# Scores of dilated attention made for two heads together, on the two halves of the partitions

## The chip, the cores and the metric

The kernel runs on one core of a Trainium2 chip. The metric is the time of one execution on the device in microseconds (us). A run is compared by the median of several executions. In the profile the engines are PE (TensorE; PEld is its loading of weights), DVE (VectorE), ACT (ScalarE), POOL (GpSimd) and SP (SyncE, which issues the DMAs).

## What is computed

A decoder trunk of two layers on 256 positions of width 1024, in float32. Each layer is

```python
h = rmsnorm(x, norm1_g[l])
z = h @ w_in[l]
out_a = dilated_mixture(qa, ka, va)          # 3 groups x 4 heads of 64, strides 1, 4, 16
out_b = diff_attention(qb, kb, vb, lam, ...) # 4 heads with two score maps each
out_c = multiscale_pool(z[..., OFF_C:OFF_G], pool_w[l], pool_scale[l])
mixed = (gates[:, :, 0] * (out_a @ w_proj_a[l])
         + gates[:, :, 1] * (out_b @ w_proj_b[l])
         + gates[:, :, 2] * (out_c @ w_proj_c[l]))
x = x + mixed @ w_out[l]
h2 = rmsnorm(x, norm2_g[l])
x = x + (swiglu(h2, ...) if l % 2 == 0 else moe_ffn(h2, ...))   # 8 experts, top 2
```

The dilated mixture makes, for each of four output heads, three maps of scores (one per group), masks them, and mixes the three softmax results by their denominators.

## The kernel before

Every weight matrix is loaded in pieces of 1 MB (tile `raw`), and each piece is split into a high part on ACT (`wh`, line 204) and a low part on DVE (`wl`, line 220). A product of float32 precision is then three matmuls of 128x128 by 128x512 (`mm3`, lines 299 to 301). Half a piece is 12 such matmuls. `run_plan` walks through a list: for each half it first converts the half that lies four ahead (`convert`), then issues the 12 matmuls, then calls `step_bg` once. All instructions of an engine run in the order in which this program writes them.

`step_bg` lets in side jobs. A side job is a generator; `bg` holds them in the order of their priority (a low number first). Each call may advance up to three of them (`st["rate"]`), each to its next `yield ready(lag, when, ...)`: it may go on after `lag` more halves, when its condition holds, and when the places that it asks for are free. The places are counted by `CAPS`: 4 PSUM buffers `tmp`, 6 probability tiles `P`, 3 transposed ones `PT`, 2 jobs of dilated attention `A`, 2 of differential attention `B`.

In a layer's mixer the plan makes the queries and keys of dilated attention first. The rotary embedding runs as a side job (`rope_T`: DVE works on `zq`, PE transposes at line 675, ACT copies to `qk` at line 679). A tile `qk` holds two heads, one on partitions 0 to 63 and one on 64 to 127. Then come the four jobs `attn_a(h)`. Each does, with a `yield` between: three blocks of `scores` (lines 698 and 699, a contraction over the 64 partitions of its half), `mask_max` (line 705, DVE), exponentials (line 711, ACT), transposes of the three probability tiles (line 716, PE), their copies to `PT` (line 721, ACT), the products with the values (lines 766 to 769, PE) and the weighted sum (lines 777 and 779, DVE). `attn_a_tail` transposes the result. Meanwhile the plan goes on through the other projections of `z`. The jobs `attn_b(h)` of differential attention follow with a lower priority; one of them makes two score maps, on the two halves of the same tiles `qk`. `attn_b_tail` takes the reciprocal root (`rsqrt`, lines 353 to 367, 12 operations of DVE on 8 columns), scales (line 875), transposes (line 882, PE) and splits (lines 309 on ACT and 315 on DVE) into `outB`. The pooling's job `pool_c` runs between them.

At the end of the mixer stand the projections of the three branches. Those of the pooling (two halves, key `outC`) and of dilated attention (one half, key `outA`) come first, for both halves of the columns, into buffers `acc`: 72 matmuls. Behind each DVE mixes the result in (line 923, or lines 926 and 928). Then `finish_bg()` issues all that is left of the side jobs, and the projection of differential attention follows into buffers `tmp`. The layer's rest (`w_out`, the norm, the dense part or the experts) depends on it.

The functions that the change touches:

Of the kernel before, what the change touches and what calls it, by code (L numbers as in the profile page):

```python
# [89 lines left out]
def trunk(ctx: ExitStack, tc: tile.TileContext, coff, cst, x, positions, norm1_g, w_in, b_gate, diff_lambda,  # L90
# [7 lines left out]
    RA, RB, WA, WB, LROPE, LC, TAB, LBT = 3, 3, 1, 2, 2, 2, 2, 1  # L98
    CAPS = {"tmp": 4, "P": 6, "PT": 3, "A": 2, "B": 2}
    AHEAD, AHEAD2 = 4, 3  # L100
# [12 lines left out]
    def tmp():  # L113
        return pp[0].tile([128, 512], F32, tag="tmp", name="tmp")
# [113 lines left out]
    def ready(lag=1, when=None, **holds):  # L228

        return lag, when, holds  # L230

    def add_bg(name, gen, prio=5):
        it = [name, gen, prio, 0, None, {}, {}]
        bg.append(it)
        bg.sort(key=lambda t: t[2])
        advance(it)

    def advance(it):
        it[5] = it[6]
        try:  # L240
            lag, when, holds = next(it[1]) or ready()
            it[3], it[4], it[6] = st["half"] + lag, when, holds
        except StopIteration:
            bg.remove(it)
# [102 lines left out]
    def small(n, name, dt=F32, bufs=2):  # L347
        return sp.tile([128, n], dt, tag=name, name=name, bufs=bufs)
# [125 lines left out]
    def first_group(ps, bank, start=False, func=None):  # L474
# [4 lines left out]
        def fn(get, j):  # L479
# [25 lines left out]
            if start:  # L505
                tables = rope_tables()
                inv_rms(lambda: next(tables))
                add_bg("tables", rest(tables), 0)
            else:
                inv_rms()  # L510
# [71 lines left out]
    def mixer(l):  # L582
        L = {}
        lam_init = 0.8 - 0.6 * math.exp(-0.3 * l)

        def mt(shape, tag, bufs=1, dt=F32):
            return (mp if tag in ("qk", "gate") else mpa).tile(shape, dt, tag=tag, name=tag, bufs=bufs)
# [69 lines left out]
        def ev_qk(key, nb):  # L657
            def f(ps):
                if L.get("rope", 0) >= 2:
                    finish_bg(f"rope{L['rope'] - 2}")  # L660
                z = mt([128, NT, 512], "zq", 2)
                to_sbuf([z[:, 0], z[:, 1]], ps)
                add_bg(f"rope{L.get('rope', 0)}", rope_T(key, nb, z), 1)
                L["rope"] = L.get("rope", 0) + 1
            return f
# [28 lines left out]
        def scores(qt, kt, par):  # L694

            r = slice(par * 64, par * 64 + 64)
            p = tmp()
            PE.matmul(p[:, 0:128], qt[r, 0:128], kt[r, 0:128], start=True, stop=True)
            PE.matmul(p[:, 128:384], qt[r, 128:256], kt[r, 0:256], start=True, stop=True)
            return p  # L700

        def mask_max(p, mask, m0, m1):
            P = mt([128, 384], "P", 6)
            for a, b, m in ((0, 128, m0), (128, 384, m1)):
                V.tensor_tensor_reduce(P[:, a:b], p[:, a:b], mask[:, a:b], 1.0, -3.0e38,
                                       op0=OP.add, op1=OP.max, accum_out=m)
            return P

        def exps(P, nm, ls):
            for (a, b), n_, s_ in zip(((0, 128), (128, 384)), nm, ls):  # L710
                S.activation(P[:, a:b], P[:, a:b], AF.Exp, bias=n_, scale=SCALE, accum_out=s_)

        def transpose3(P):
            p = tmp()
            for j in range(3):
                PE.transpose(p[:, j * 128:(j + 1) * 128], P[:, j * 128:(j + 1) * 128], ident)
            return p

        def evac3(p):
            t = mt([128, 384], "PT", 3)  # L720
            S.activation(t, p[:, :384], AF.Copy)
            return t

        def attn_a(h):
            yield ready(0, lambda: len(L.get("qa", [])) == 6, tmp=3, A=1)
            pr, par = divmod(h, 2)
            if h == 0:
                L["oa"] = mt([128, NT, 256], "oa")
            ps = []
            for g in range(3):  # L730
                hq, hk = 4 * g + h, AH + 4 * g + h
                ps.append(scores(L["qa"][hq // 4][:, (hq // 2) % 2], L["qa"][hk // 4][:, (hk // 2) % 2], par))
            L["nA"] = L.get("nA", 0) + 1
            yield ready(1, P=3, A=1)
            m = small(6, "am")
            P = [mask_max(ps[g], masks[g], m[:, g:g + 1], m[:, 3 + g:4 + g]) for g in range(3)]
            m3 = m.rearrange("p (i g) -> p i g", g=3)
            M = small(2, "aM")
            V.tensor_reduce(M, m3, axis=AX.X, op=OP.max)
            nm = small(6, "anm")  # L740
            V.tensor_scalar(nm, m, -SCALE, None, op0=OP.mult)
            d = small(6, "ad")
            V.tensor_tensor(d.rearrange("p (i g) -> p i g", g=3), m3, M[:, :, None].to_broadcast([128, 2, 3]), op=OP.subtract)
            yield ready(1, P=3, A=1)
            ls = small(6, "al")
            for g in range(3):
                exps(P[g], [nm[:, g:g + 1], nm[:, 3 + g:4 + g]], [ls[:, g:g + 1], ls[:, 3 + g:4 + g]])
            e = small(6, "ae")
            S.activation(e, d, AF.Exp, scale=SCALE)
            yield ready(WA, tmp=3, A=1)  # L750
            pts = [transpose3(P[g]) for g in range(3)]
            yield ready(1, PT=3, A=1)
            pts = [evac3(p) for p in pts]
            w = small(6, "aw")
            V.tensor_tensor(w, e, ls, op=OP.mult)
            den = small(2, "aden")
            V.tensor_reduce(den, w.rearrange("p (i g) -> p i g", g=3), axis=AX.X, op=OP.add)
            V.reciprocal(den, den)
            c = small(6, "ac")
            V.tensor_tensor(c.rearrange("p (i g) -> p i g", g=3), e.rearrange("p (i g) -> p i g", g=3),  # L760
                            den[:, :, None].to_broadcast([128, 2, 3]), op=OP.mult)
            yield ready(1, tmp=1, A=1)
            o = tmp()
            for g in range(3):
                v = L["va"][:, :, (4 * g + h) * 64:(4 * g + h + 1) * 64]
                PE.matmul(o[:, g * 64:g * 64 + 64], pts[g][:, 0:128], v[:, 0], start=True, stop=True)
                ob = o[:, 192 + g * 64:256 + g * 64]
                PE.matmul(ob, pts[g][:, 128:256], v[:, 0], start=True, stop=False)
                PE.matmul(ob, pts[g][:, 256:384], v[:, 1], start=False, stop=True)
            yield ready()  # L770
            for i in range(NT):
                dst = L["oa"][:, i, h * 64:(h + 1) * 64]
                for g in range(3):
                    src = o[:, i * 192 + g * 64:i * 192 + (g + 1) * 64]
                    cc = c[:, i * 3 + g:i * 3 + g + 1]
                    if g == 0:
                        V.tensor_scalar(dst, src, cc, None, op0=OP.mult)
                    else:
                        V.scalar_tensor_tensor(dst, src, cc, dst, op0=OP.mult, op1=OP.add)

        def attn_a_tail():
            yield ready(1, lambda: not any(pending(f"A{h}") for h in range(4)), tmp=1)
            L["outA"] = pieces(mp, "qk", 10, 2)
            p = tmp()
            for k in range(2):
                for i in range(NT):
                    PE.transpose(p[:, k * 256 + i * 128:k * 256 + (i + 1) * 128],
                                 L["oa"][:, i, k * 128:(k + 1) * 128], ident)
            yield ready()
            split(*L["outA"].pieces[0], p.rearrange("p (k t) -> p k t", k=2))  # L790
# [147 lines left out]
        for b in range(3):  # L938
            z_block(b * 512, 512, ev_qk("qa", b))
            if b == 0:  # L940
                do(loads)
                do(lambda: add_bg("lam", lam(), 1))
                if l == DEPTH - 1:
                    do(router_loads)
            if b == 2 and l == DEPTH - 1:
                do(router_consts)
# [1 line left out]
        z_block(OFF_VA + 512, 256, ev_nat("va", 768, 512))  # L948

        def start_a():  # L950
            for h in range(4):
                add_bg(f"A{h}", attn_a(h), 3)
            add_bg("Atail", attn_a_tail(), 3)
            st["rate"] = RA

        def start_b():
# [3 lines left out]
            st["rate"] = RB  # L960

        do(start_a)
        z_block(OFF_QB, 512, ev_qk("qb", 0))
        z_block(OFF_KB, 512, ev_qk("kb", 0))
# [636 lines left out]
    masks = []  # L1601
# [91 lines left out]
```

## Time and profile before

| | |
|---|---|
| median of 3 runs | 1717.09 us (1716.28 to 1717.39) |
| the profiled execution | 1715.65 us, span 1713.9 us |
| PE busy | 1638.7 us, 96% of the span |
| DVE busy | 972.3 us, 57% |
| ACT busy | 798.4 us, 47% |
| DMA | 489.06 MB, mean 285 GB/s |

The span runs from the first to the last instruction. The first layer's mixer lies in about the first 275 us, the dense part up to 520, the second layer's mixer up to 775, and the experts behind it, with the DMA queues at about 400 GB/s.

### The profile page before, as it was taken

Reading aid. Unit: us, or ns where it says so; the run is one execution under the profiler, and the core shown is the slowest. Engines: PE = TensorE matmul, PEld = TensorE weight load, DVE = VectorE, ACT = ScalarE, POOL = GpSimd, SP = SyncE. Lnnn points to the kernel's source line nnn. Section 1 sums busy time; section 2 is a strip of 40 time slices with the busy share of each in tenths; the row PEclk is TensorE's granted clock in tenths of the full one; section 3 lists DMA queues with packets and bytes.
Section 4 is the critical chain, followed back from the end, with each engine's and each line's share of the span. In section 5 each row is a group of like instructions: output and inputs, shape, how many; then the busy total and the mean of one; then the engine's idle time right before and its main releaser. Section 6 shows DMA issues by size and latency. Waiting matters only on the chain. (4 is left out here: it accounts for less than half of the span.)

```text
span 1713.9 us, 24266 instructions
## 1 busy us (share of the span) xinstructions
PE 1638.7 (96%) x7753; PEld 1178.1 (69%) x7753; DVE 972.3 (57%) x1415; ACT 798.4 (47%) x994; POOL 3.1 (0%) x6
## 2 busy tenths in 40 slices
PE   9999999999999999998999999999999999999895
PEld 6878888888888888785575654766646666467464
DVE  6556686545456556684472644744536556257376
ACT  6555544443345555533452633635325544145362
POOL 0000000000000000000000000000000000000000
PEclk9999999999999999998999999999999999999997
DMA  8435555554546535485999989999899999999890
GB/s 270 165 123 168 171 185 194 178 205 170 198 153 194 172 126 164 159 319 221 410 410 407 407 339 413 406 399 405 335 411 403 399 407 374 381 411 410 327 398 28
DMA packets 161694, 489.06 MB, mean 285 GB/s; under 512 B 13424, under 2 KB 18672, under 8 KB 147440
## 3 DMA queue, kind: packets, MB, share of 16 engines
q1 hardware_dynamic: 161520, 486.86, 75.4%
q8 instruction: 94, 1.54, 0.4%
q14 instruction: 80, 0.66, 0.1%
HBM read 485.78 MB, written 1.05 MB: 284 GB/s over the span
## 5 line engine op out<-in xcount | busy, mean ns | idle before, releaser
L220 DVE TENSOR_TENSOR wl<-raw,wh 128x1024 fp32r<-128x1024 f32 (+1 forms) x407 | 671.0, 1670 | 347.1 <-ACT wh L204 328.4
L204 ACT ACTIVATE wh<-raw 128x1024 fp32r<-128x1024 f32 (+1 forms) x407 | 563.9, 1416 | 298.6 <-PE gu L301 78.6
L299 PE MATMUL acc<-wl,hTh 128*128 128x512 f32 (+1 forms) x544 | 218.7, 402 | 1.2 <-DVE wl L220 1.1
L301 PE MATMUL acc<-wh,hTl 128*128 128x512 f32 (+1 forms) x544 | 212.0, 390 | 0.4 <-DVE hTl L315 0.4
L300 PE MATMUL acc<-wh,hTh 128*128 128x512 f32 (+1 forms) x544 | 211.6, 389 | 0.0
L299 PE MATMUL gu<-wl,xg 128*128 128x512 f32 x448 | 180.9, 404 | 28.7 <-DVE wl L220 20.7
L1385 PE MATMUL gu<-raw,xf 128*64 128x512 f32 (+1 forms) x1016 | 200.8, 543 | 4.9 <-PEq L1301 4.9
L301 PE MATMUL gu<-wh,xg 128*128 128x512 f32 x448 | 177.4, 396 | 0.0
L300 PE MATMUL gu<-wh,xg 128*128 128x512 f32 x448 | 177.4, 396 | 0.0
L1385 PEld LDWEIGHTS gu<-raw,xf 128*64 128x64 f32 x1016 | 70.7, 137 | 110.6 <-issue 97.7
L299 PEld LDWEIGHTS gu<-wl,xg 128*128 128x128 f32 x448 | 84.6, 189 | 65.2 <-ACT wh L204 23.1
L299 PEld LDWEIGHTS acc<-wl,hTh 128*128 128x128 f32 x544 | 102.5, 188 | 27.1 <-issue 4.6
L301 PEld LDWEIGHTS acc<-wh,hTl 128*128 128x128 f32 x544 | 102.4, 188 | 24.2 <-DVE hTl L315 0.9
L300 PEld LDWEIGHTS acc<-wh,hTh 128*128 128x128 f32 x544 | 102.7, 189 | 20.3
L1385 PE MATMUL y<-raw,af 128*64 128x512 f32 x448 | 101.1, 596 | 0.0
L301 PEld LDWEIGHTS gu<-wh,xg 128*128 128x128 f32 x448 | 84.7, 189 | 20.0
L299 PE MATMUL y<-wl,aT 128*128 128x512 f32 x224 | 90.2, 403 | 8.0 <-DVE wl L220 7.2
L300 PEld LDWEIGHTS gu<-wh,xg 128*128 128x128 f32 x448 | 84.8, 189 | 18.2
L299 PE MATMUL tmp<-wl,cols 128*128 128x512 f32 x240 | 95.8, 399 | 0.0
L301 PE MATMUL tmp<-wh,cols 128*128 128x512 f32 x240 | 95.2, 397 | 0.0
L300 PE MATMUL tmp<-wh,cols 128*128 128x512 f32 x240 | 95.1, 396 | 0.0
L301 PE MATMUL y<-wh,aT 128*128 128x512 f32 x224 | 88.5, 395 | 0.0
(258 smaller groups left out, 1740.7 us busy)
## 6 DMA issues: line engine op xcount, KB each, us to landing
raw<-in_moe_w_up SPq DMA_DIRECT2D x112, 1024.0 KB, 10.7
raw<-in_moe_w_gate SPq DMA_DIRECT2D x111, 1024.0 KB, 11.2
raw<-in_moe_w_down SPq DMA_DIRECT2D x110, 1024.0 KB, 11.4
raw<-in_w_in SPq DMA_DIRECT2D x57, 1024.0 KB, 5.1
raw<-in_ffn_w_gate SPq DMA_DIRECT2D x14, 1024.0 KB, 5.2
raw<-in_ffn_w_up SPq DMA_DIRECT2D x14, 1024.0 KB, 5.2
raw<-in_ffn_w_down SPq DMA_DIRECT2D x14, 1024.0 KB, 5.1
raw<-in_w_out SPq DMA_DIRECT2D x8, 1024.0 KB, 5.2
```

Source lines behind the costliest of these rows:

```text
L204: S.activation(hi, raw_t[u][0][:, o:o + n], AF.Copy)
L220: V.tensor_tensor(lo, raw, hi.bitcast(F32), op=OP.subtract)
L299: PE.matmul(ps, xh, wl, start=start, stop=False)
L300: PE.matmul(ps, xh, wh, start=False, stop=False)
L301: PE.matmul(ps, xl, wh, start=False, stop=stop)
L1385: PE.matmul(ps[j * 64:j * 64 + 64, cols.start + o:cols.start + o + g], w, raw[:, kk, o + j * g:o + j * g + g], start=fst, stop=lst)
```

## The change

`scores_a(h)` for h = 0 and 2 makes the scores of heads h and h + 1 in turn for each of the three groups, two at a time, with a `yield` after each pair, and masks each pair one step later. It asks for both places `A` and for six tiles `P` in the end. When all three pairs are masked it adds the two jobs `attn_a(h, P, m)`, which go on from the maxima as before. `add_bg` lets a new job hold places from its start.

```diff
-    def add_bg(name, gen, prio=5):
+    def add_bg(name, gen, prio=5, **holds):
+
         it = [name, gen, prio, 0, None, {}, {}]
         bg.append(it)
         bg.sort(key=lambda t: t[2])
         advance(it)
+        it[5] = holds
...
-        def attn_a(h):
-            yield ready(0, lambda: len(L.get("qa", [])) == 6, tmp=3, A=1)
-            pr, par = divmod(h, 2)
+        def scores_a(h):
+
+            yield ready(0, lambda: len(L.get("qa", [])) == 6, tmp=2, A=2)
             if h == 0:
                 L["oa"] = mt([128, NT, 256], "oa")
-            ps = []
+            m = [small(6, "am") for _ in range(2)]
+            P = [[], []]
             for g in range(3):
                 hq, hk = 4 * g + h, AH + 4 * g + h
-                ps.append(scores(L["qa"][hq // 4][:, (hq // 2) % 2], L["qa"][hk // 4][:, (hk // 2) % 2], par))
-            L["nA"] = L.get("nA", 0) + 1
-            yield ready(1, P=3, A=1)
-            m = small(6, "am")
-            P = [mask_max(ps[g], masks[g], m[:, g:g + 1], m[:, 3 + g:4 + g]) for g in range(3)]
+                ps = [scores(L["qa"][hq // 4][:, (hq // 2) % 2], L["qa"][hk // 4][:, (hk // 2) % 2], j) for j in range(2)]
+                yield ready(1, P=2 * g + 2, tmp=2 if g < 2 else 0, A=2)
+                for j in range(2):
+                    P[j].append(mask_max(ps[j], masks[g], m[j][:, g:g + 1], m[j][:, 3 + g:4 + g]))
+            L["nA"] = L.get("nA", 0) + 2
+            for j in range(2):
+                add_bg(f"A{h + j}", attn_a(h + j, P[j], m[j]), 3, P=3, A=1)
+
+        def attn_a(h, P, m):
...
-            for h in range(4):
-                add_bg(f"A{h}", attn_a(h), 3)
+            for h in (0, 2):
+                add_bg(f"A{h}", scores_a(h), 3)
```

The program has as many instructions on PE as before, and those of SP and POOL stand in the same order. Side jobs move. In the rows of the changed program the lines stand 2 further down than before up to `start` of the dilated jobs (the scores are lines 700 and 701), and 7 further behind it (the scaling is line 882, the transposes 889).

**TensorE at the first scores** (`acc` is an ordinary projection, `tmp<-qk` a score map; a map is a row of 128 and a row of 256 columns). Before:

```order
L301 MATMUL acc<-wh,hTl 128x512
L698 MATMUL tmp<-qk 128x128
L699 MATMUL tmp<-qk 128x256
L698 MATMUL tmp<-qk 128x128
L699 MATMUL tmp<-qk 128x256
L698 MATMUL tmp<-qk 128x128
L699 MATMUL tmp<-qk 128x256
L299 MATMUL acc<-wl,hTh 128x512
```

And with the change:

```order
L303 MATMUL acc<-wh,hTl 128x512
L700 MATMUL tmp<-qk 128x128
L701 MATMUL tmp<-qk 128x256
L700 MATMUL tmp<-qk 128x128
L701 MATMUL tmp<-qk 128x256
L301 MATMUL acc<-wl,hTh 128x512
```

Before, a block is three maps of one head, and there are four such blocks in a layer. Now a block is two maps, of two heads, and there are six. Differential attention's maps, which stood in one block of four and two of two, now stand in four of two.

**ScalarE at the probabilities of the first two heads** (`P,al` are the exponentials of a head, `PT` the copies of transposed probabilities, `wh` conversions). Before:

```order
L749 ACTIVATE ae<-ad 128x6
L204 ACTIVATE wh<-raw 128x1024
L655 ACTIVATE zq<-acc,rr_267 128x512 x2
L711 ACTIVATE P,al<-P,anm 128x128
L711 ACTIVATE P,al<-P,anm 128x256
L711 ACTIVATE P,al<-P,anm 128x128
L711 ACTIVATE P,al<-P,anm 128x256
L711 ACTIVATE P,al<-P,anm 128x128
L711 ACTIVATE P,al<-P,anm 128x256
L749 ACTIVATE ae<-ad 128x6
L204 ACTIVATE wh<-raw 128x1024
L721 ACTIVATE PT<-tmp 128x384 x3
```

And with the change:

```order
L756 ACTIVATE ae<-ad 128x6
L713 ACTIVATE P,al<-P,anm 128x128
L713 ACTIVATE P,al<-P,anm 128x256
L713 ACTIVATE P,al<-P,anm 128x128
L713 ACTIVATE P,al<-P,anm 128x256
L713 ACTIVATE P,al<-P,anm 128x128
L713 ACTIVATE P,al<-P,anm 128x256
L756 ACTIVATE ae<-ad 128x6
L204 ACTIVATE wh<-raw 128x1024 x2
L681 ACTIVATE qk<-tmp 128x512
L723 ACTIVATE PT<-tmp 128x384 x3
```

The exponentials of the second head now follow those of the first at once, and two conversions and the copy of rotated queries (line 681) stand between them and the first head's copies.

**VectorE at the end of the first mixer** (`rr` is the reciprocal root's result, `nat<-gate,acc` and the pairs `gate`, `nat` mix a branch in, `zq<-zq,rr` is the scaling ahead of the transposes, `cols<-tmp,sg` the low part behind them). Before:

```order
L367 TENSOR_SCALAR rr_2026<-rr_2026 128x8
L220 TENSOR_TENSOR wl<-raw,wh 128x1024
L875 TENSOR_TENSOR zq<-zq,rr_2026 128x512 x2
L220 TENSOR_TENSOR wl<-raw,wh 128x1024
L923 SCALAR_TENSOR_TENSOR nat<-gate,acc 128x512 x2
L220 TENSOR_TENSOR wl<-raw,wh 128x1024
L926 SCALAR_TENSOR_TENSOR gate<-gate,acc 128x512
L928 TENSOR_TENSOR nat<-nat,gate 128x512
L926 SCALAR_TENSOR_TENSOR gate<-gate,acc 128x512
L928 TENSOR_TENSOR nat<-nat,gate 128x512
L315 SCALAR_TENSOR_TENSOR cols<-tmp,sg,cols 128x512
```

And with the change:

```order
L369 TENSOR_SCALAR rr_2124<-rr_2124 128x8
L220 TENSOR_TENSOR wl<-raw,wh 128x1024
L933 SCALAR_TENSOR_TENSOR gate<-gate,acc 128x512
L935 TENSOR_TENSOR nat<-nat,gate 128x512
L933 SCALAR_TENSOR_TENSOR gate<-gate,acc 128x512
L935 TENSOR_TENSOR nat<-nat,gate 128x512
L882 TENSOR_TENSOR zq<-zq,rr_2124 128x512 x2
L317 SCALAR_TENSOR_TENSOR cols<-tmp,sg,cols 128x512 x2
```

Before, the four mixing operations shown are those of the first half of the columns. With the change they are those of the second half, behind the last matmuls into `acc`; the mixing of the second pooled half, four rows for two sums of squares and the other 11 operations of the root stand right ahead of the first row shown. On TensorE the 8 transposes, which stood in two blocks of 4 with 24 matmuls into `acc` between them and 24 behind, now stand in one block, behind all matmuls into `acc` and right ahead of those into `tmp`. The product of the last head with the values stands 36 matmuls ahead of that block; it stood 48 ahead of the first block and 96 ahead of the matmuls into `tmp`.

## Rows read from the trace of the kernel before

**Rows 1.** Busy time by windows: both mixers; granted clock, DMA share and GB/s last.
```profile
55.00:245.00 190.00, 188.00 (x961) 153.70 (x960) 120.87 (x303) 102.42 (x205) 0.00 (x0) 1.00 0.48 158
520.00:760.00 240.00, 238.00 (x1191) 194.31 (x1190) 155.62 (x386) 134.51 (x250) 0.00 (x0) 1.00 0.56 188
```

**Rows 2.** Timeline of PE (start, length), three maps of one head.
```profile
69.01 0.40 PE L301 MATMUL acc<-wh,hTl 128*128 128x512 f32 x1
69.33 0.48 PE L698 MATMUL tmp<-qk 64*128 64x128 f32 x2
...
71.83 0.40 PE L300 MATMUL acc<-wh,hTh 128*128 128x512 f32 x1
```

**Rows 3.** Timeline of PE: two pairs in one block, then one pair alone.
```profile
139.76 0.40 PE L301 MATMUL acc<-wh,hTl 128*128 128x512 f32 x1
...
142.03 0.39 PE L300 MATMUL acc<-wh,hTh 128*128 128x512 f32 x1
...
176.03 0.40 PE L301 MATMUL acc<-wh,hTl 128*128 128x512 f32 x1
176.35 0.50 PE L698 MATMUL tmp<-qk 64*128 64x128 f32 x4
...
177.55 0.39 PE L300 MATMUL acc<-wh,hTh 128*128 128x512 f32 x1
```

**Rows 4.** Waits of PE: total, times and longest in us.
```profile
PE tmp L716 <- ACT PT L721: 3.6, 4, 1.1
```

**Rows 5.** Timeline of ACT: exponentials, conversion, copies.
```profile
83.17 0.39 ACT L711 ACTIVATE P<-P,anm 128x128 f32<-128x128 f32 x1
...
85.91 1.04 ACT L204 ACTIVATE wh<-raw 128x1024 fp32r<-128x1024 f32 x1
86.86 1.22 ACT L721 ACTIVATE PT<-tmp 128x384 f32<-128x384 f32 x3
```

**Rows 6.** Timeline of DVE at the end of the first mixer.
```profile
217.76 0.28 DVE L866 CUSTOM_DVE_ANT_0 bscr<-zq 128x128 f32<-128x128 f32 x1
...
218.30 0.17 DVE L353 TENSOR_SCALAR rv<-bssq 128x8 f32<-128x8 f32 x1
...
220.60 1.23 DVE L220 TENSOR_TENSOR wl<-raw,wh 128x1024 fp32r<-128x1024 f32 x1
221.75 1.29 DVE L875 TENSOR_TENSOR zq<-zq,rr 128x512 f32<-128x512 f32 x2
...
224.09 1.28 DVE L923 SCALAR_TENSOR_TENSOR nat<-gate,acc 128x512 f32<-128x512 f32 x2
...
226.42 0.68 DVE L926 SCALAR_TENSOR_TENSOR gate<-gate,acc 128x512 f32<-128x512 f32 x1
...
229.07 0.74 DVE L315 SCALAR_TENSOR_TENSOR cols<-tmp,sg,cols 128x512 fp32r<-128x512 f32 x1
```

**Rows 7.** Timeline of PE there, and of ACT in the last row.
```profile
217.83 0.39 PE L300 MATMUL acc<-wh,cols 128*128 128x512 f32 x1
...
222.28 0.40 PE L301 MATMUL acc<-wh,cols 128*128 128x512 f32 x1
222.58 0.30 PE L882 MATMUL tmp<-ident,zq 128*128 128x128 f32 x1
223.09 0.55 PE L882 MATMUL tmp<-ident,zq 128*128 128x128 f32 x3 [0.21 <-DVE zq L875]
...
223.71 0.40 PE L300 MATMUL acc<-wh,cols 128*128 128x512 f32 x1
...
229.10 0.60 PE L882 MATMUL tmp<-ident,zq 128*128 128x128 f32 x4
...
229.74 0.69 ACT L309 ACTIVATE cols<-tmp,sg 128x512 fp32r<-128x512 f32 x1 [1.20 <-PE tmp L882]
```

**Rows 8.** A stretch among the experts: timeline of PE, then a window (clock 0.50).
```profile
1626.65 0.50 PE L299 MATMUL gu<-wl,xg 128*128 128x512 f32 x1 [3.87 <-DVE wl L220]
...
1628.20:1631.50 3.30, 3.30 (x9) 2.56 (x8) 3.04 (x2) 2.16 (x2) 0.00 (x0) 0.50 1.02 408
```

## The prediction

> **What bounds the kernel now.** I first read the busy time by stretches, for the two attention layers [rows 1]: TensorE is busy for 188.00 of 190 us in the first and 238.00 of 240 us in the second, at the full granted clock of 1.00, while VectorE and ScalarE are busy for little more than half of it and the DMA queues for 0.48 and 0.56. So in the stages that the change touches TensorE sets the time, and two things count: what a side job costs on TensorE's stream, and where TensorE waits. The order in time of TensorE's instructions came next. The ordinary projection matmuls start 0.2345 us apart: nineteen steps from 217.83 to 222.28 [rows 7]. Where a side job is let in, I take as its cost the time from the start of the last ordinary matmul before it to the start of the second one behind it, less two such steps. Last I read VectorE's and ScalarE's order at the end of the mixer, since a wait of TensorE must come from there.
>
> **The scores.** A block of three scores of one head (one half of the partitions) costs 71.83 − 69.01 − 0.47 = 2.35 us [rows 2]. A head of dilated attention has one such block, so a layer pays 4 × 2.35 = 9.4 us. The differential attention already makes its scores in pairs on both halves: one pair costs 177.55 − 176.03 − 0.47 = 1.05 us, and two pairs in one block 142.03 − 139.76 − 0.47 = 1.80 us [rows 3]. So the second pair adds 0.75 us, 0.38 us per score where a lone head pays about 0.7, and entering a block costs about 0.3 us. The change makes the same call with the same operands' shape, so I take the pair's price: six blocks of one pair, 6 × 1.05 = 6.3 us, a gain of 3.1 us per layer. Differential attention, pushed along, stands in four blocks of one pair instead of one of two and two of one: 4.20 against 1.80 + 2.10 = 3.90, 0.3 us lost. Net: **2.8 us less per layer**. Bounds: no overlap at all gives six blocks of two lone scores, 6 × (0.3 + 1.4) = 10.2 us, that is 0.8 + 0.3 = 1.1 us lost; no price for entering gives a gain of 4.6 us.
>
> The Trainium skill (TensorEngine Tiling (Array Packing), Overview and Tiling Modes) promises up to twice the speed for a contraction of 64, but says that a change of tiling mode drains TensorE. Rows 2 and 3 agree with both: 0.38 us against 0.7 us, and 0.3 us for each entry. By the doubling alone the gain would be 4.7 us per layer, an estimate from that page; with the drain it is the 2.8 us above.
>
> **The transposes of the probabilities.** Of four heads' transposes two wait now for a PSUM buffer, until ScalarE has copied out the head before: 3.6 us in four waits, 1.8 us per layer, the longest 1.1 [rows 4]. ScalarE's order now puts one head's exponentials (83.17 to 85.91, 2.74 us) and one conversion (1.04 us) ahead of the copies, 0.41 us each [rows 5]; after the change both heads' exponentials and two conversions stand there. If TensorE begins the first head's transposes when its exponentials end, the second head's first buffer is free 2.74 + 2 × 1.0 + 0.5 = 5.2 us later, where TensorE asks for it after about 1.0 + 12 × 0.2345 = 3.8 us: a wait of 1.4 us for the first two heads, with a copy of rotated queries ahead of it about 1.8. For the other two a 1.3 us job of the pooling lies between, so some 0.5 us. Sum 2.3 against 1.8 us: **0.5 us more per layer**. The bounds are no wait (1.8 us less) and three times the wait of now (3.6 us more).
>
> **The end of differential attention.** This is the term that decides. Before, the last head's product with the values stands 96 matmuls ahead of the projection that needs it, and the 8 transposes lie in two blocks among the projections of the other branches. The change takes the pairs of heads one after the other: the second pair of dilated heads needs both places of the first, and six probability tiles, so differential attention starts later and alternates. Now the last head's product stands 36 matmuls ahead of that projection, and the tail is forced out at its door. What counts is VectorE's order there: mixing in of the second pooled half, the last sums of squares, the 12 small operations of the reciprocal root, a conversion, four mixing operations for the projection just ended, and only then the scaling, for which the transposes wait. Let E be the start of the first matmul slot behind the last projection of branch A. The second mixing operation needs a result from 12 matmuls earlier, there at E − 2.81 − 0.23 + 0.40 = E − 2.65. From there, with lengths from [rows 6]:
> - mixing 0.64 (half of 1.28), squares 0.54 (217.76 to 218.30), root 2.30 (to 220.60): E + 0.83;
> - conversion 1.15 (to 221.75), four mixing operations 2.65 (226.42 to 229.07): E + 4.63;
> - scaling: TensorE began the first transpose 0.83 us and the others 1.34 us after its start (222.58 and 223.09 against 221.75) [rows 6, 7]: E + 5.46 and E + 5.97;
> - ScalarE's high part begins 0.64 us after the transposes (229.10 to 229.74) and takes 0.69, so the first two products can go at about E + 7.2; VectorE's low part takes 0.74, so the third goes at E + 7.95.
>
> The stream thus goes on as if it had begun at 7.95 − 0.47 = E + 7.5 us. Before, the two transpose blocks cost 223.71 − 222.28 − 0.47 = 0.96 us with a wait of 0.5 in it, and 0.45 us [rows 7], together 1.4. Net: **6.1 us more per layer**. Nothing hides it, since all later work on TensorE in the layer hangs on the same projection's sums. The operations are the old ones; their cover was the 96 matmuls, 22.5 us. Bounds: if conversion and squares are already done, 1.7 us less; if the first mixing is late because a conversion before it waits for its weights, some 1.2 us more.
>
> **The clock.** TensorE sits idle for 5.3 us there and then works in pieces. The one idle stretch of this length in the trace, 3.87 us, was followed by a stretch of 3.30 us at a granted clock of 0.50, the lower level of 1.2 GHz; work begun at 1626.65 had run on at full clock until then [rows 8]. At half clock each us of dense work gives away 0.5 us, so 3.3 us cost 1.65 if it is all dense. The earliest part may fall into the wait, so I take **1.5 us per layer**; bounds 0 and, for twice that stretch, 3.3.
>
> **Sum.** Per layer −2.8 + 0.5 + 6.1 + 1.5 = +5.3 us, for two layers +10.6 us. The other instructions are the same in number, on SP and POOL in the same order. The expert stage behind is fed by buffers that are full by then and starts later by the same amount. The profiled execution took 1715.65 us (span 1713.9), so 1726.2; the median of the three runs is 1.44 us above it, and the sum from it is **1727.7 us**. About 0.2%, 3.4 us, is what a measurement of this kernel tells from no change.
>
> **Rivals.**
> - The tail waits, but the clock stays at 1.00 because the transposes break the idle time: 2 × 3.8 = +7.6, 1724.7 us. For it: the waits of 1.1 us [rows 4] did not lower the clock, which is 1.00 over both layers [rows 1]. Against: 5.3 us is longer than 3.87. Chance 0.22.
> - The clock falls for longer, or a second wait appears behind the late conversions: another 2 to 4 us per layer, 1732 to 1736 us. For it: VectorE is two conversions behind when the stream goes on. Against: conversions run four halves ahead, 48 matmuls or 11 us. Chance 0.13.
> - The tail is hidden, and the kernel is faster: if VectorE reaches the scaling before E, only −2.8 + 0.5 per layer is left, −4.6, 1712.5 us. It takes a chain shorter by 5 us; from a tail of less than 2.3 us per layer on, the change wins. For it: VectorE has 64% of work in the stage [rows 1]. Against: the order of its queue is fixed and two of its steps wait for TensorE itself. Chance 0.05.
> - Half of the tail is hidden and the clock stays: about 2 × 0.8 us, 1718.7, the same. Chance 0.05.
> - The pairs do not overlap here: 1.1 us lost instead of 2.8 gained per layer, 1735.5 us. Against: the same function's pairs in [rows 3]. Chance 0.03.
>
> **The numbers.** The forecast has 0.52. Its own bounds reach from about 1721 to 1734; the range of 1720.5 to 1734 leaves out the faster and the same case, and the far end of the longer drop, about 2 in 10. Faster by over 0.2%: 0.06, within it 0.08, slower 0.86.
>
> **What would show it.** Right: score blocks of one pair at about 1.05 us; TensorE idle for some 5 us ahead of the 8 transposes at the end of each mixer, released by VectorE's scaling; a granted clock of 0.50 for some 3 us behind it; the expert stage unchanged in length. Wrong: transposes that start within 2 us of the last projection of branch A; score blocks of 1.7 us; or waits elsewhere in the mixer, ahead of the probability transposes above all.

## The result, and the profile after

The changed kernel takes 1725.88 us (median of 5 executions, 1723.85 to 1727.07) where the kernel before took 1716.49 on the same chip (5 executions, 1716.25 to 1717.39): a ratio of 1.0055 [1.0043, 1.0066], slower by 9.4 us. Forecast were +10.6 us and 1727.7 us.

The profiled execution took 1726.53 us with a span of 1724.7 us, 10.9 above that of before (1724.75 against 1713.87). Where the time goes is read from the start of the n-th matmul in one trace against the n-th in the other, taken at places where the programs are in step again (times are those of the kernel before). This lag is −0.2 us ahead of the first mixer, +4.4 behind it (at 241 us), +4.3 ahead of the second (565), +9.3 behind that (743), +9.7 at 1569 and +11.8 near the end (1660). So nearly all of it arises in the two mixers, 4.6 and 5.0 us; the last 60 us give about 0.9 back.

Busy time by windows in the changed kernel: the stretches of [rows 1], then three short ones (granted clock third from the end).

```profile
55.00:245.00 190.00, 182.90 (x937) 147.12 (x936) 117.91 (x298) 101.34 (x203) 0.00 (x0) 0.98 0.48 156
520.00:760.00 240.00, 232.90 (x1167) 187.67 (x1166) 151.18 (x381) 130.11 (x245) 0.00 (x0) 0.99 0.53 173
233.60:240.30 6.70, 3.75 (x12) 2.79 (x13) 4.77 (x8) 2.20 (x3) 0.00 (x0) 0.50 0.00 0
742.20:748.90 6.70, 4.63 (x14) 3.47 (x15) 4.66 (x7) 3.08 (x4) 0.00 (x0) 0.50 0.00 0
1636.50:1643.20 6.70, 5.77 (x14) 4.51 (x15) 5.46 (x3) 3.74 (x3) 0.00 (x0) 0.50 1.03 411
```

TensorE was idle for 2.0 of those 190 us before and is idle for 7.1 of them now. The waits of TensorE in the changed kernel (total, times, longest) say for whom, beside [rows 4]:

```profile
PE tmp L889 <- DVE zq L882: 10.6, 2, 5.3
...
PE tmp L718 <- ACT qk L681: 2.5, 2, 1.2
...
PE tmp L718 <- ACT PT L723: 1.0, 2, 0.5
```

The transposes at the end of differential attention wait 5.3 us in each layer for VectorE's scaling. The timeline of TensorE in the changed kernel, at a pair of maps (beside [rows 2, 3]), at the wait of 5.3 us ([rows 7]), and among the experts ([rows 8]):

```profile
68.85 0.40 PE L303 MATMUL acc<-wh,hTl 128*128 128x512 f32 x1
69.17 0.50 PE L700 MATMUL tmp<-qk 64*128 64x128 f32 x4
69.50 0.61 PE L701 MATMUL tmp<-qk 64*128 64x256 f32 x4
70.04 0.50 PE L301 MATMUL acc<-wl,hTh 128*128 128x512 f32 x1
70.37 0.39 PE L302 MATMUL acc<-wh,hTh 128*128 128x512 f32 x1
...
230.80 0.39 PE L303 MATMUL acc<-wh,cols 128*128 128x512 f32 x1
236.49 2.27 PE L889 MATMUL tmp<-ident,zq 128*128 128x128 f32 x8 [5.30 <-DVE zq L882]
238.68 0.80 PE L301 MATMUL tmp<-wl,cols 128*128 128x512 f32 x1
239.27 0.63 PE L302 MATMUL tmp<-wh,cols 128*128 128x512 f32 x1
239.70 0.63 PE L303 MATMUL tmp<-wh,cols 128*128 128x512 f32 x1
...
1637.43 0.79 PE L301 MATMUL gu<-wl,xg 128*128 128x512 f32 x1 [4.93 <-DVE wl L220]
```

A pair costs 70.37 − 68.85 − 0.47 = 1.05 us. The last matmul of branch A starts at 230.80, so E, the slot behind it, is 231.03; the transposes begin at E + 5.46. What VectorE does until then, by its own timeline in the changed kernel (beside [rows 6]):

```profile
228.42 0.69 DVE L930 SCALAR_TENSOR_TENSOR nat<-gate,acc 128x512 f32<-128x512 f32 x1 [0.72 <-PE acc L303]
229.03 0.28 DVE L873 CUSTOM_DVE_ANT_0 bscr<-zq 128x128 f32<-128x128 f32 x1
...
229.57 0.17 DVE L355 TENSOR_SCALAR rv<-bssq 128x8 f32<-128x8 f32 x1
...
231.86 1.22 DVE L220 TENSOR_TENSOR wl<-raw,wh 128x1024 fp32r<-128x1024 f32 x1
233.00 0.68 DVE L933 SCALAR_TENSOR_TENSOR gate<-gate,acc 128x512 f32<-128x512 f32 x1
...
235.65 1.29 DVE L882 TENSOR_TENSOR zq<-zq,rr 128x512 f32<-128x512 f32 x2
238.66 1.60 DVE L317 SCALAR_TENSOR_TENSOR cols<-tmp,sg,cols 128x512 fp32r<-128x512 f32 x2 [1.72 <-ACT cols L311]
```

From 228.42, where it had waited for TensorE itself, VectorE works without a gap to the scaling at 235.65: mixing, squares, root, conversion, four mixing operations. In TensorE's order nothing stands between the last projection and the transposes, so nothing fills the wait.

### The profile page after: what moved, and what is told of

It reads as the page before. It is cut to its first block, busy times and chain, and to the rows that moved or that the text cites. A ratio compares the mean times of both kernels' runs of the same rounds, so it can differ in the third digit from the quotient of the medians.

```text
span 1724.7 us, 24251 instructions
## 1 busy us (share of the span) xinstructions
PE 1639.7 (95%) x7753; PEld 1174.8 (68%) x7753; DVE 972.6 (56%) x1415; ACT 798.2 (46%) x994; POOL 3.1 (0%) x6
## 3 DMA queue, kind: packets, MB, share of 16 engines
HBM read 485.78 MB, written 1.05 MB: 282 GB/s over the span
## 6 DMA issues: line engine op xcount, KB each, us to landing
raw<-in_moe_w_up SPq DMA_DIRECT2D x112, 1024.0 KB, 10.9
```

## The experiments

Lags are against the kernel before, from the profiled executions, as above. The length of a stretch at half clock is read from a trace's record of the granted clock. The cost of a block on TensorE is counted as in the prediction.

**Both heads' maps from the same half of the partitions** (e1_one_half). Heads 1 and 3 get the maps of heads 0 and 2, and theirs are left out; the number, shape and place of the instructions stay.

```diff
-                ps = [scores(L["qa"][hq // 4][:, (hq // 2) % 2], L["qa"][hk // 4][:, (hk // 2) % 2], j) for j in range(2)]
+                ps = [scores(L["qa"][hq // 4][:, (hq // 2) % 2], L["qa"][hk // 4][:, (hk // 2) % 2], 0) for j in range(2)]
```

> The changed kernel, with the scores of both heads of a pair taken from partitions 0 to 63, so that nothing can overlap; heads 1 and 3 of dilated attention then get the scores of heads 0 and 2. Theory (the two halves work at the same time): a block of two maps costs 2.35 - 0.66 = about 1.7 us instead of 1.05, twelve blocks in two layers, +7.8 us against the changed kernel, near 1733.7 us; the idle time ahead of the 8 transposes stays 5.3 us. Rival (what a pair saves is only the entering of a block, or the order in which the maps stand): the blocks stay at 1.05 us and the time at 1725.9.

Measured: 1731.45 us, ratio 1.0087 [1.0072, 1.0102], against 1.0055 of the changed kernel. The timeline of TensorE in this kernel, at a pair:

```profile
70.79 0.40 PE L303 MATMUL acc<-wh,hTl 128*128 128x512 f32 x1
71.12 0.49 PE L700 MATMUL tmp<-qk 64*128 64x128 f32 x2
...
72.62 0.51 PE L301 MATMUL acc<-wl,hTh 128*128 128x512 f32 x1
72.97 0.39 PE L302 MATMUL acc<-wh,hTh 128*128 128x512 f32 x1
```

The pair costs 72.97 − 70.79 − 0.47 = 1.71 us instead of 1.05. Twelve pairs of dilated heads in two layers make 7.9 us; the mixers add 17.0 us of lag here (from +1.8 to +18.8) and 9.5 in the changed kernel, 7.5 more, and the two medians, each by its ratio, are 5.5 us apart. The idle time ahead of the last transposes is unchanged, 5.30 and 5.29 us. So the halves do run beside each other, and that gain is in the changed kernel's time. The Trainium skill (TensorEngine Tiling (Array Packing), Tiling Modes) says that different tiles can execute matmuls in parallel; the size here is 0.66 us for two maps.

**Scaling ahead of the last mixing** (e2_scale_first). The changed kernel, with the last branch's four mixing operations issued behind the scaling and the low parts. The rest of the edit puts these operations into a function of their own.

```diff
...
         for n in range(2):
             proj(n, 2, w_proj_c, "outC", acc)
-            proj(n, 0, w_proj_a, "outA", acc)
+            proj(n, 0, w_proj_a, "outA", acc, late=late if n else None)
         do(finish_bg)
+        do(lambda: late[0]())
```

> The changed kernel, with the mixing of the last projection into acc (4 operations of VectorE, 2.65 us) issued behind the scaling and the low parts instead of ahead of them. Theory (VectorE's queue sets the tail): TensorE's idle time ahead of the 8 transposes falls from 5.3 to 2.65 us, 5.3 us less in two layers, and up to 2 us more where the clock now stays at full: 1718.5 to 1720.6 us. Rival (the tail is set by the last head's own chain, from its product with the values on): idle time and 1725.9 us unchanged.

Measured: 1718.80 us (10 executions), ratio 1.0020 [1.0011, 1.0029]. The timelines of TensorE and of VectorE in this kernel:

```profile
233.96 0.30 PE L889 MATMUL tmp<-ident,zq 128*128 128x128 f32 x1 [2.65 <-DVE zq L882]
...
235.79 0.50 PE L301 MATMUL tmp<-wl,cols 128*128 128x512 f32 x1 [0.34 <-ACT cols L311]
```

```profile
233.13 1.29 DVE L882 TENSOR_TENSOR zq<-zq,rr 128x512 f32<-128x512 f32 x2
...
237.10 0.68 DVE L939 SCALAR_TENSOR_TENSOR gate<-gate,acc 128x512 f32<-128x512 f32 x1
```

The idle time falls by 5.30 − 2.65 = 2.65 us, the length of the four operations, in both layers. The order of VectorE's queue is what TensorE waits for; the 2.65 us that are left belong to the mixing, squares, root and conversion, which still stand ahead of the scaling. The clock stayed at full in the first layer and fell for 3.41 us in the second (windows of this kernel); the lags behind the mixers are +1.1 and +2.7 us.

```profile
231.00:238.00 7.00, 3.76 (x18) 2.39 (x17) 5.43 (x13) 2.95 (x4) 0.00 (x0) 1.00 0.02 5
738.20:741.60 3.40, 3.30 (x11) 2.42 (x12) 1.58 (x3) 1.76 (x3) 0.00 (x0) 0.51 0.00 0
```

**Work for TensorE in the wait** (e4_junk). The changed kernel, with 44 matmuls of zeros ahead of the transposes, whose result is not used.

```diff
             L["outB"] = pieces(mp, "qk", 10, 4)
+            warm(22)
```

> The changed kernel, with 44 matmuls of zeros (128x256, bf16, into a PSUM buffer that nothing reads) ahead of the 8 transposes in each mixer, so that TensorE works through the wait for VectorE. Theory (the wait lowers the granted clock, and that costs about 1 us per layer on top): the transposes start when they did, the granted clock stays at 1.00 in both mixers, 2 us less than the changed kernel, about +7.5 us against the kernel before. Rival (the clock's drop costs nothing, since it falls into the wait): unchanged at about +9.5 us.

Measured: 1722.43 us, ratio 1.0038 [1.0023, 1.0053]. The timeline of TensorE and a window of this kernel:

```profile
230.83 4.98 PE L346 MATMUL tmp<-junk 128*128 128x256 bf16 x44
236.28 0.30 PE L890 MATMUL tmp<-ident,zq 128*128 128x128 f32 x1 [0.47 <-DVE zq L882]
```

```profile
231.00:241.00 10.00, 8.93 (x63) 6.98 (x62) 8.35 (x15) 3.62 (x5) 0.00 (x0) 1.00 0.00 1
```

No half clock is left in either mixer, and the chain of VectorE is as long as it was. Over both mixers the lag grows by 7.4 us (from −0.35 to 7.05) where it grows by 9.4 in the changed kernel (from −0.16 to 9.27): the half clock costs 2.0 us, **1.0 us per layer** (0.8 in the first, 1.2 in the second). The intervals of the two ratios overlap, so this rests on the traces.

**The kernel before, with its tail made late** (e5_before_late). No pairs; `WB`, the lag ahead of two steps of the jobs `attn_b`, goes from 2 to 3, so that the transposes are forced at the door of the last projection.

```diff
-    RA, RB, WA, WB, LROPE, LC, TAB, LBT = 3, 3, 1, 2, 2, 2, 2, 1
+    RA, RB, WA, WB, LROPE, LC, TAB, LBT = 3, 3, 1, 3, 2, 2, 2, 1
```

> The kernel before (lone heads), with a lag of 3 instead of 2 halves at the same two places (WB): the 8 transposes are forced at the projection's door as in the changed kernel, but the last product stands 48 matmuls ahead, and on VectorE the scaling stands ahead of the last mixing, the low part behind it. Theory (VectorE's order sets the tail): no idle time ahead of the transposes; the third product waits for the low part, which comes after a conversion 1.15, mixing 2.65 and itself 0.74 from the scaling's end at about E - 0.8, so at E + 3.8 us, the stream goes on at E + 3.3 against 1.4 us for the two blocks before: +1.9 us per layer, 1720.3 us. Rival (forcing the tail at the door costs 6 to 7 us whatever stands on VectorE): 1729 to 1731 us.

Measured: 1726.06 us, ratio 1.0052 [1.0036, 1.0067], some 5 to 6 us above what was expected. The timelines of TensorE and of VectorE:

```profile
233.19 0.40 PE L301 MATMUL acc<-wh,cols 128*128 128x512 f32 x1
...
235.96 0.40 PE L300 MATMUL tmp<-wh,cols 128*128 128x512 f32 x1
238.75 0.80 PE L301 MATMUL tmp<-wh,cols 128*128 128x512 f32 x1 [2.39 <-DVE cols L315]
```

```profile
235.30 0.68 DVE L926 SCALAR_TENSOR_TENSOR gate<-gate,acc 128x512 f32<-128x512 f32 x1
...
237.95 1.40 DVE L315 SCALAR_TENSOR_TENSOR cols<-tmp,sg,cols 128x512 fp32r<-128x512 f32 x2
```

Here the scaling stands ahead of the last mixing, so the transposes do not wait; the low part stands behind it, and the third product waits 2.39 us for that. It starts at E + 5.3 (E is 233.19 + 0.23 here), where E + 3.8 was expected: the scaling was put to end before E and starts at 232.96, behind the mixing of the second pooled half (231.76), so the low part comes 1.5 us later. A clock of 0.50 followed too, for 6.83 us in the first layer and 3.41 in the second, which the expectation had left out. A late tail alone, with no pairs, makes a kernel as slow as the changed one.

**An earlier tail** (e3_wb1, e7_rate5). In the changed kernel, e3_wb1 lowers `WB` from 2 to 1; e7_rate5 lets each call of `step_bg` advance 5 jobs instead of 3 (`RA`, `RB`).

> The changed kernel, with a lag of 1 instead of 2 halves at two places of each differential attention job (WB), which puts its last product 84 matmuls ahead of the projection that needs it instead of 36. Theory (the pairs gain 2.7 us per layer, the tail and its clock take 7): no idle time ahead of the transposes, no clock of 0.50 in the mixers, 2 x 2.7 us less than the kernel before, 1711 us, and 1710 to 1712.5 with the waits for PSUM buffers. Rival (moving the side jobs costs elsewhere, the pairs' gain is eaten): 1716.5 us or more.

> The changed kernel with five side jobs per half (RA, RB) and the lags as they were: the last product stands 84 matmuls ahead, the transposes 36 and 12 ahead, but on VectorE the mixing of the first pooled half, which waits for TensorE, stands ahead of the scaling. Theory (VectorE's order sets the tail): idle time of 1.4 us ahead of the first transposes, as with the lag of 1, no other wait of the tail, the single transposes without a wait: -2 to -3 us against the kernel before. Rival (the lag, not VectorE's order, made the wait of the run with WB 1): no idle time there and -5 us.

Measured: 1717.60 us, ratio 1.0008 [0.9999, 1.0017], and 1723.42 us (4 executions, 1719.28 to 1727.66), ratio 1.0052 [1.0035, 1.0069]. Neither gave the gain that was expected. The timelines of TensorE and VectorE in e3_wb1, then the waits of e7_rate5:

```profile
224.01 0.40 PE L303 MATMUL acc<-wh,cols 128*128 128x512 f32 x1
225.83 0.30 PE L889 MATMUL tmp<-ident,zq 128*128 128x128 f32 x1 [1.42 <-DVE zq L882]
```

```profile
223.80 1.28 DVE L930 SCALAR_TENSOR_TENSOR nat<-gate,acc 128x512 f32<-128x512 f32 x2
225.00 1.29 DVE L882 TENSOR_TENSOR zq<-zq,rr 128x512 f32<-128x512 f32 x2
```

```profile
PE tmp L773 <- DVE oa L786: 3.3, 2, 1.6
PE tmp L889 <- DVE zq L882: 3.2, 4, 1.4
```

Now the mixing of the first pooled half, which itself needs a product of TensorE, stands ahead of the scaling: the transposes come earlier than VectorE again, by 1.4 us. In the first layer of e3_wb1 that block costs 1.5 us more than before, and two blocks with transposes of P in differential attention 0.5 and 0.6 more (1.86 and 0.95 instead of 1.38 and 0.33 in the changed kernel); together they are the pairs' whole gain, and the lag behind that mixer is what it was ahead of it, +0.4. At rate 5 the last dilated head's products with the values (line 773; the expectations call it the third, by its number) also wait 1.64 us in each layer, released by VectorE's weighted sum of the head before. The profiled execution of e7_rate5 took 1719.28 us, the lowest of its four; what made the other three longer stays open.

**All three numbers together** (e6_early_b, e8_late_rate, e9_rate_pv, e10_late_mix). `WB` 1, `LBT` (the lag ahead of the transposes) 2, and rate 4: in e6_early_b from the start, in e8_late_rate from the end of dilated attention on, in e9_rate_pv from the last head's products on; in both it ends with the tail. e10_late_mix is e8_late_rate with the edit of e2_scale_first. The edit of e6_early_b:

```diff
-    RA, RB, WA, WB, LROPE, LC, TAB, LBT = 3, 3, 1, 2, 2, 2, 2, 1
+    RA, RB, WA, WB, LROPE, LC, TAB, LBT = 4, 4, 1, 1, 2, 2, 2, 2
```

> The changed kernel with four instead of three side jobs per half (RA, RB), WB 1 and a lag of 2 halves ahead of the tail's transposes (LBT): the last product stands 120 matmuls ahead of the projection, the transposes 60 and 36 ahead, and on VectorE scaling and low part stand ahead of the last mixing. Theory (pairs gain 2.7 us per layer and only late differential attention takes it back): no idle time ahead of the tail's transposes, no clock of 0.50 in the mixers, small waits of up to 1 us per layer at the single transposes left by the short lag: -3.5 to -5.4 us against the kernel before, 1711 to 1713 us. Rival (the pairs bring nothing that can be had in the whole): within 1 us of the kernel before.

> The changed kernel with WB at 1 and LBT at 2 as in e6_early_b, but the background advances three items a halfstep until the dilated attention's tail is done and four from there to the end of the differential attention. Theory: the third head's products of P and V stand where they stood in the changed kernel, so the wait of 1.64 us ahead of them is gone, the tail of the differential attention stays without a long wait of TensorE and without half clock, and the pairs' 2.7 us a layer remain, less about 0.5 us a layer for waits at the four score blocks of the differential attention, whose steps follow one another more closely: -2.2 a layer, -4.4 in all, 1711 to 1712 us, ratio 0.997 to 0.998, if the expert stage is as before; up to 1.7 us more if a half-clock stretch there is longer, as in e3_wb1. Rival (the wait ahead of the products is not from the rate but from the order of the exponentials on ScalarE): the wait stays, and the time is that of e6_early_b, 1714 us, ratio 0.999.

> As e8_late_rate, but the rate goes from three to four right behind the fourth dilated head's products with the values, and back to three behind the tail of the differential attention. TensorE's order of the dilated attention is that of the changed kernel; the differential attention's maps stand in two blocks of two pairs, as in the kernel before, and its transposes in two blocks with 24 ordinary matmuls between and 72 behind. Theory (the tail's place in VectorE's order is all that the pairs lose): no wait ahead of the products of P and V, none ahead of the tail's transposes, none at the third product, no half clock in the mixers; 2.7 us a layer from the dilated pairs and 0.6 from the differential blocks, less at most 0.5 for a wait at the six transposes: -2.8 to -3.3 a layer, 1710 to 1711 us, ratio 0.996 to 0.997. Rival (each step nearer moves the wait to the next place, as in e7_rate5): a new wait of 1 to 2 us a layer ahead of a block of transposes or of products, 1713 to 1715 us, ratio 0.998 to 0.999.

> As e8_late_rate, with the last branch's four mixing operations issued behind the low parts, as in e2_scale_first. Theory: in e8_late_rate the wait of 1.33 us at the third product of the differential projection came from the low part's place behind those four operations on VectorE; with it ahead of them the wait goes, 1.3 to 1.5 us a layer, and the waits of 0.5 and 0.6 us at the differential transposes stay: 1713 us, ratio 0.998. Rival (the conversions ahead of the low part are what is late): no change against e8_late_rate, 1715.7 us, ratio 1.000.

| | median us | ratio | lag behind the mixers, us | largest new wait, us |
|---|---|---|---|---|
| e6_early_b | 1713.84 | 0.9992 [0.9983, 1.0001] | −1.8, −3.0 | 1.64 at the products of the probabilities P with the values V |
| e8_late_rate | 1715.73 | 1.0000 [0.9991, 1.0009] | +0.3, +0.3 | 1.33 at the third product |
| e9_rate_pv | 1715.69 | 1.0002 [0.9993, 1.0011] | 0.0, −0.3 | 1.14 at transposes of P |
| e10_late_mix | 1714.85 | 0.9995 [0.9986, 1.0004] | +0.8, +0.1 | 0.64 at the transposes of the mixed columns |

The lags start from −0.6, +0.4, 0.0 and +1.6 us ahead of the first mixer. One fence each: the timeline of TensorE in e6_early_b and in e9_rate_pv, the waits of TensorE in e8_late_rate, and the timeline of TensorE in e10_late_mix:

```profile
144.84 1.02 PE L821 MATMUL tmp<-gate,pw 128*128 128x256 f32 x4
147.51 0.43 PE L773 MATMUL tmp<-va,PT 128*128 128x64 f32 x2 [1.64 <-DVE oa L786]
...
218.44 0.60 PE L889 MATMUL tmp<-ident,zq 128*128 128x128 f32 x4
```

```profile
152.08 0.49 PE L700 MATMUL tmp<-qk 64*128 64x128 f32 x2 [0.38 <-DVE oa L788]
...
171.00 1.49 PE L718 MATMUL tmp<-ident,P 128*128 128x128 f32 x6 [1.14 <-DVE P L859]
```

```profile
PE tmp L303 <- DVE cols L317: 2.7, 2, 1.3
```

```profile
234.70 0.60 PE L890 MATMUL tmp<-ident,zq 128*128 128x128 f32 x4
235.06 0.48 PE L301 MATMUL tmp<-wl,cols 128*128 128x512 f32 x1
```

In all four the wait ahead of the last transposes is gone, and so is the half clock in the mixers: the loss is repaired. The pairs' 2.7 us per layer do not appear in full, because each of these schedules puts another step of TensorE ahead of VectorE's or ScalarE's part in it. e6_early_b came out between its theory and its rival, 1.4 us below the kernel before by its ratio. In e8_late_rate the theory was right about the products of P and V (no wait) and wrong about the tail: the wait moved to the low part. In e9_rate_pv the rival was right: waits in the block of two pairs (2.99 us instead of 1.81 before) and at the transposes of P (blocks of 2.62 and 1.24, with 0.65, 0.33 and 0.33 before) use up the gain. e10_late_mix removed the wait that it was to remove and got 0.7 us a layer beside e8_late_rate, where 1.3 to 1.5 were expected: TensorE is idle for 0.64 us ahead of the transposes of the mixed columns, which need the late mixing. None of these versions beats the kernel before by more than its interval.

## Why the prediction was right, step by step

- **Scores.** Forecast −2.8 us per layer, measured 10.53 instead of 13.26 us in all score blocks of a layer, −2.7. A pair costs the 1.05 us of [rows 3]; e1_one_half shows that it is 0.66 us dearer without the second half.
- **Transposes of the probabilities.** Forecast +0.5, measured +0.1: the four blocks cost 6.36 instead of 6.29 us, without the jobs that stand in one block with them. This term was mis-sized: the first two heads' wait is 1.22 us where 1.8 was worked out. The row names the copy of rotated queries, which the prediction had too, but only as a delay of the first head's copies to `PT`; in the trace TensorE goes on as soon as that copy has freed its buffer, ahead of those copies (0.41 us each). The second wait, 0.5, is as forecast.
- **The tail.** The deciding step. Forecast: second mixing at E − 2.65, scaling at E + 4.63, transposes at E + 5.46; measured E − 2.61, E + 4.62, E + 5.46. The block of transposes costs 8.00 us, and the first matmuls behind it, at half clock, another 0.51; less the 1.4 of before that is +7.1 for tail and clock together, against 6.1 + 1.5 forecast. e2_scale_first shows that the chain on VectorE is the cause, and e5_before_late that it needs no pairs.
- **Clock.** Forecast a drop of about 3.3 us, worth 1.5. It lasts 6.83 us in both layers, but the first 2.9 us of it in the first layer (233.57 to 236.49) and 2.0 in the second (742.2 to 744.2) fall into the idle time; by e4_junk it costs 0.8 in the first layer, which leaves 6.3 there for the tail. The length was forecast at half of what it was, and that the cost still came out near is partly luck: the idle time took up a part of the drop.
- **Sum.** −2.7 + 0.1 + 7.1 = +4.5 us per layer, with +5.3 forecast and 4.6 and 5.0 read from the lags. The second layer's 0.4 more go with its half clock (1.2 instead of 0.8 us by e4_junk).
- **Expert stage.** "Unchanged in length" is right up to 1569 us, where the lag has grown by 0.4 since 743. In this execution one wait behind it is then 4.93 instead of 3.87 us [rows 8], and the half clock around it 6.83 instead of 3.41 us long; the two together make the lag grow by another 2.3 us. In the traces of the ten experiments the stretch there is 3.41 us in e1, e2, e4, e8 and e9 and 6.83 in e3, e5, e6, e7 and e10, with and without a late tail. So whether it belongs to the change stays open; the medians' 9.4 us are close to the mixers' part alone, and the profiled execution's 10.9 comes as near to the forecast's 10.6 only through this stage.

## What to carry to other kernels

Before side jobs are made denser or regrouped, look for the last of them whose result the main stream needs, and write out in order what stands ahead of its inputs on the engine that finishes it: here a gain of 2.7 us on TensorE was paid with 7 us because 36 matmuls (8.4 us) were left as cover where 96 had been. VectorE took its operations in the program's order at this place in every timeline shown, so moving the four cheap operations that nobody waits for yet behind the one that is waited for takes back two thirds of the loss. What remains then has to be found wait by wait, and a gain of this size can be lost again in waits of 0.5 to 1.6 us.

## What the hardware showed that was not expected

An idle time of TensorE in the mixer came with a granted clock of 0.50, the lower level of 1.2 GHz, in some places and not in others of the same length: 5.3 us by one of 6.83 us, begun within the idle time, in all four cases (the changed kernel and e1_one_half, two layers each), 2.65 us (e2_scale_first) by none in the first layer and 3.41 us in the second, 2.39 us (e5_before_late) by 6.83 and 3.41 us, and 1.42 us (e3_wb1) by none in the first layer and by 3.41 us, begun 1.4 us after work had gone on, in the second; 1.41 us in e7_rate5 was followed by none in either, nor was 1.64 us in e6_early_b and e7_rate5. A short wait can thus cost more than its length, and not in every layer alike.
